# A two-block layer: where scan, gated unit and half of a projection stand among the attention heads

## The chip, the cores and the metric

The kernel runs on one core of one Trainium2 chip. The number that counts is the device time of one execution in microseconds (us), as the median over runs. The kernel is one program: a first transformer block (feed-forward, token mix, feed-forward) and a second block (attention and a state-space scan side by side, then a feed-forward with a convolution). 512 tokens of 1024 features; all in fp32, where most products are made as three products of high and low parts (fp32r).

## The reference, cut to what matters

The change touches only the middle of the second block:

```python
o_attn = nsa_attention(...)     # 8 heads of 64: 512 features; two dense causal branches and a compressed one, gated
y_ssm = s5_mixer(...)           # 512 features
    # inside: x = associative_scan(...); y = C x + d_skip * u
    #         y = gelu(y); y = y * sigmoid(y @ w_glu + b_glu)
mix = concatenate([rmsnorm(o_attn, attn_norm_g), rmsnorm(y_ssm, ssm_norm_g)], axis=-1)
x = x + gt1 * (mix @ w_o)
h = rmsnorm(x, norm2_g) * (1.0 + sc2) + sh2
u = causal_dwconv(h @ w_up, conv_w, conv_b)      # ... the feed-forward follows
```

Features 0 to 511 of `mix` are the attention's (k-tiles 0 to 3 of `w_o`), features 512 to 1023 the state-space output's (k-tiles 4 to 7).

## The kernel before, in words

Tiles are feature-major: 128 features on the partitions, 512 tokens in the free dimension. A weight block is loaded on the SP queue into `wraw`, copied to `whi` on ScalarE (L200) and subtracted to `wlo` on VectorE (L201); `mm3` then makes, for each k-tile, the products hi x hi (L212) and hi x lo (L213), and last lo x hi (L215).

The order of the instructions on each engine is made beforehand by a scheduler. Code order is an instruction's rank; `rank(-150)` moves what it encloses 150 places ahead. Tiles in SBUF and PSUM come from pools; a tile that reuses bytes waits for the earlier users of these bytes.

PSUM has banks of three kinds: four "a", two "p", two "t". In the attention, scan banks ("s") and a head pair's output bank ("o") are both of kind "p" (`self.kinds = dict(s="p", o="p")`). Scores, the gated unit's sums and the projection's sums are "a"; the transposed probabilities and the norm's row sums are "t".

`attn_heads` goes over four pairs of heads; each has two branches `br`. A branch computes, for two heads, scores (L1899) in a bank, their maximum (L1902), the exponential (L1908), a scaling by the gate on GpSimd (L1915), transposes (L1918), copies out (L1923, L1925) and at its end products with the values into `po` (L1931, L1936). After both branches `po` is copied to `oT` (L1938).

`s5_scan` is a generator with two steps for each quarter of the groups. A quarter loads its constants, copies its input to `z3` (L1608), transposes it (L1611, bank `pt`), copies it (L1613), multiplies (L1623, bank `pin`), rotates and scans on VectorE (L1628 to L1641), multiplies (L1652, bank `py`), adds (L1654), transposes back (L1657, another `pt`) and copies to `yT` (L1658). All four banks are "s".

Before the change `between(p)` runs one quarter ahead of each pair:

```python
for p in range(4):
    between(p)                 # next(s5); next(s5); at p == 3 also closes the scan's pool
    po = self.bank("o", [N, T])
```

After all pairs comes, under `rank(-150)`, the gated unit `glu`: gelu of four tiles (L2003), their split (L1231, L1232), four blocks of 12 products of 512 columns with `w_glu`, each with a sigmoid (L2010) and a product (L2011), and then the norm of the gated output (`mix2_norm` with `g_ssm`: squares L361, sums L363, L369, root L390, reciprocal L391, rows L379 and L381, scaling L1951, split L1231 and L1232).

`block2_merge` makes the same norm of the attention's output, and then `out_proj`: for the two halves of 256 tokens, eight output tiles `n`; each takes 24 products of 256 columns (k-tiles 4 to 7 first), a residual update (L1304), a square and a sum for the next norm (L361, L363). The weights of two tiles are held between the halves, so 14 blocks of 512 KB are loaded and split. After each half come the next norm's rows and the modulated operands (L422, L423), and the feed-forward's first products (L480, L481, L484).

Of the kernel before, what the change touches and what calls it, by code (L numbers as in the profile page):

```python
# [18 lines left out]
KT = 8  # L19
# [119 lines left out]
class Net:  # L139
# [16 lines left out]
    def pool(self, **k):  # L156
        """A pool whose tiles wait only for the earlier users of their own bytes."""
        if k.get("space") != bass.MemoryType.DRAM:
            k["reuse_waits"] = "tile"
        return self.tc.tile_pool(**k)  # L160
# [24 lines left out]
    def bank(self, group, shape=(128, 512)):  # L185
        """A PSUM bank of a kind: "a" (four), "p" and "t" (two each); self.kinds maps other names of a phase to them."""
        k = self.kinds.get(group, group)
        return self.pp.tile(list(shape), F32, tag=k, name=self.nm("ps" + group), bufs=dict(a=4, p=2, t=2)[k])
# [18 lines left out]
    def mm3(self, ps, w, x, last=0):  # L207
        """ps = sum_k w[k]^T x[k]; w, x: lists of (hi, lo) operand pairs over k-tiles. The low parts of w
        (or of x, with last=1) come into play last."""
# [12 lines left out]

    def ada_dot(self, w, ci):
        """sum_k c[k] * w[:, k] over the k-tiles of a [128, KT, 256] block: still to be summed over partitions."""
        nc = self.nc
        acc = self.tp.tile([128, 256], F32, tag="adaacc", name=self.nm("adaacc"), bufs=3)
        nc.vector.tensor_scalar(acc, w[:, 0], self.cs[:, ci, 0:1], None, ALU.mult)
        for k in range(1, KT):
            nc.vector.scalar_tensor_tensor(acc, w[:, k], self.cs[:, ci, k : k + 1], acc, ALU.mult, ALU.add)  # L229
        return acc  # L230

    def ada_dot2(self, w, ci, pool):
        """The same with products on ScalarE and sums on GpSimd."""
# [14 lines left out]
    def ada_finish(self, accs, outs, bias, chunk, b, tag):  # L248
        """Column sums over partitions, plus bias: outs[i][:, 2b : 2b + 2]."""
# [9 lines left out]
    def ada_product(self, w, outs, bias, chunk, b, tag):  # L259
        """Modulations by the first two vectors of c from a [128, KT, 256] block, with TensorE: outs[i][:, 2b : 2b + 2]."""  # L260
# [13 lines left out]
    def block_sum(self):  # L274
        """A stationary operand that sums over the partitions p with the same p % 32."""
# [5 lines left out]
    def ada_steps(self, src, bias, jobs, tag, done=None):  # L281
        """Small steps of the modulation vectors: jobs are (chunk, cids, outs); done(chunk) after its last block."""
# [9 lines left out]
        def sums(acc, part):  # L292
            """Sums over groups of 32 partitions, those partitions then being the columns within a group."""
# [4 lines left out]
        def finish(c, part, outs):  # L298
            """Sums over the groups of partitions, plus bias: outs[i] over all blocks."""
# [32 lines left out]
    def rank(self, n):  # L332
        """Instructions that the scheduler is to rank n places lower (higher if negative)."""
# [15 lines left out]

    def ssq(self, width, pool=None, tag="tok"):  # L350
        """Running sum of squares over features; see ssq_add and ssq_rstd."""
# [3 lines left out]
    def ssq_add(self, st, src, sl, k, eng=None, scale=1.0):  # L355
        """Adds k-tile k (columns sl)."""
# [8 lines left out]
    def ssq_cols(self, st, sl, ps):  # L365
        """Sums over features, tokens on partitions: one column of ps for each 128 tokens of sl."""
# [7 lines left out]
    def token_rows(self, rs, cols, sl, ps):  # L374
        """rs[:, sl] = the values of cols (tokens on partitions) along every partition."""
# [7 lines left out]
    def ssq_rstd(self, st, sl, ps):  # L383
        """1 / rms of columns sl, on every partition."""
# [15 lines left out]
    def new_xm(self, es):  # L400
        """Space for the (hi, lo) pairs of the modulated norm of x."""
# [8 lines left out]
    def norm_tile(self, xm, x, rs, a, sh, k, sl, pool=False):  # L410
        """(hi, lo) of (x * rs) * a + sh for k-tile k, columns sl."""
# [14 lines left out]
    def norm_mod(self, xm, xr, rs, a, sh, sls, dve=(0, 2, 4, 6)):  # L426
        """Operand pairs of the modulated norm, by column ranges in the order of sls."""
# [12 lines left out]
    def ffn(self, segs, w_in, w_out, act=None, group0=None, tail=None, nlast=2):  # L440
        """segs: (xm pairs over k, width, residual tiles, gate): residual += gate * swiglu(xm).
        group0: PSUM tiles of the first group when its products are already issued.
        tail(si, n, sl): called as the last group updates columns sl of residual tile n."""
# [17 lines left out]
        def stage_in(gi):  # L461
            hs = [[] for _ in segs]
            for jj, j in enumerate((gi * 2, gi * 2 + 1)):
# [8 lines left out]
                if j == 0:  # L472
                    # column halves and k-tiles in the order in which the norm delivers them
# [41 lines left out]
        def finish(gi, hs):  # L515
            """Output of the last nlast groups, by column halves, each with its tail."""
# [72 lines left out]
    def ffn1_start(self, xm, cm, segs, sp):  # L589
        """Modulation, norms and the first group's products, in steps of two k-tiles as the weights arrive."""  # L590
# [32 lines left out]
        # the square root's table is loaded while x arrives  # L623
# [12 lines left out]
        # the context's two accumulators of a bank share one group, opened by a product with zeros  # L636
# [53 lines left out]

    def mix_consts(self):
        """Masks of the two-level causal structure."""
# [34 lines left out]
    def gate_bounds(self):  # L727
        """Per-channel constants of the gates."""
# [21 lines left out]
    # fm column tiles of mix_fm  # L750
# [6 lines left out]
    def proj(self, w, seg, halves=False, tag="p"):  # L757
        """Feature-major projection of a segment ('x' or 'c') into a PSUM tile."""
# [7 lines left out]
    def vproj(self, src, bias, pool, tag, ones_col, nbs=range(4), bufs=6):  # L766
        """Token-major values: list of 6 chunk tiles [128 tok, heads, 128 (+2)]."""
# [40 lines left out]
    def hgrn_dir(self, h, d, q):  # L808
        """Gates of one head and direction; returns reference-shifted q, k, block products, ctx k, ctx/full decays."""
# [19 lines left out]
        def two(t, i0, i1):  # L829
            """Slots (i0, i1) of the inner index, in that order."""  # L830
# [31 lines left out]
        # block products: pre (ahead of the block's shifted reference) and suf (behind it), per level  # L862
# [23 lines left out]
        # context keys decayed to the end of the scan  # L886
# [12 lines left out]
    def hgrn_head(self, h, v):  # L899
# [18 lines left out]
        # mixed operands per level: half-blocks where the forward (backward) pairs live  # L918
# [36 lines left out]
        # states ahead of each chunk  # L955
# [43 lines left out]
    def mlstm_rows(self, rp):  # L999
        """Gate recurrences on rows (0:8 forward heads, 32:40 backward heads in reversed time)."""  # L1000
# [57 lines left out]
        # token-major scalars  # L1058
# [16 lines left out]
        # rows of M, natural time, as an exact hi + lo pair  # L1075
# [11 lines left out]
        # decays per (pair, direction, step), broadcast to the partitions of each head  # L1087
# [136 lines left out]
    def split(self, pool, tag, src, bufs):  # L1224
        """Exact hi + lo pair of a [128, T] tile."""
# [8 lines left out]
    def mix_heads(self, w):  # L1234
        """Normed, gated heads, feature-major: hi/lo pairs of hm and hh."""
# [54 lines left out]
    def out_proj(self, name, xs, gate, a, sh, ks=range(KT)):  # L1290
        """Residual += gate * (W xs), then its modulated norm, by column halves."""
# [3 lines left out]
        for sl in self.HALVES:  # L1295
            # the second half begins with the weights that the first one ended with
            for i, n in enumerate((6, 7, 0, 1, 2, 3, 4, 5) if sl.start else range(KT)):
                h, l = held.pop(n) if n in held else self.weights(self.ins[name][n], [KT, 128])
# [65 lines left out]
    def final_rstd(self, st, sl):  # L1364
        """For y = x * g / rms(x): 1 / rms(x), and 1 / (rms(x) * rms(y)) = 1 / sqrt(m2 + eps * (m1 + eps)),
        with m1, m2 the mean squares of x and x * g."""
# [33 lines left out]

    def s5_tables(self, w, tag):
        """Per group, for chunks of 8 steps: input, output and within-chunk matrices, and the rotation of the
        chunk-to-chunk recurrence; parked in DRAM. States lie on partitions, two groups to a tile."""
# [40 lines left out]
        def cmul(o, a, b):  # L1444
            """o = a * b for small complex pairs; o may not alias."""
# [9 lines left out]
        # f = (a - 1) / lam  # L1455
# [16 lines left out]
        # C as (real, -imaginary), each group's channels padded to 32 columns  # L1472
# [12 lines left out]
        # rotation tables e^(i 8 theta j)  # L1485
# [33 lines left out]
        # a^(7-t) B, a^(t+1) C on (state, step, channel)  # L1519
# [58 lines left out]
    def s5_scan(self, z2, wl, yT):  # L1578
        """z2: inputs [64 chunks, 8 steps, 512] in DRAM; writes gelu(S5(z)) feature-major into yT[4] ([128, T]).
        A generator: one quarter of the groups per step."""  # L1580
# [23 lines left out]
        for q in range(4):  # L1604
# [38 lines left out]
            # the groups of a pair lie on different parts of the array, and run side by side  # L1643
# [28 lines left out]
    def rope(self, ps, w):  # L1672
        """Rotary embedding of a feature-major tile (two heads of 64)."""
# [11 lines left out]
    def vtok2(self, nb, pool=None):  # L1685
        """Token-major projection of 256 columns: after its weights, two PSUM tiles [128, 2 chunks, 256]."""
# [12 lines left out]
    def token_pairs(self, x, w):  # L1699
        """[128 (2 heads x 64), T] with even and odd tokens on the two halves of the partitions."""  # L1700
# [7 lines left out]
    def compress(self, xk, xv, w):  # L1708
        """Block MLPs of token pairs: transposed hidden activations [128, 2, 128] (keys, then values from column 64)
        and the second layers' weights. The first layers lie on different columns of the array, and run side by side."""  # L1710
# [31 lines left out]
    def attn_operands(self, wl, w):  # L1742
        """Operands that the attention of all heads needs."""
# [5 lines left out]
        # keys and values of the two dense branches  # L1749
# [14 lines left out]
        # compressed keys and values  # L1764
# [318 lines left out]
```

## Time and profile before

| what | before |
|---|---|
| median of 3 runs (lowest, highest) | 2657.37 us (2654.51, 2658.23) |
| span of the profiled execution | 2655.4 us |
| busy, PE (TensorE) | 2548.3 us (96%) |
| busy, PEld (weight load, beside PE) | 2160.2 us (81%) |
| busy, DVE (VectorE) | 1671.0 us (63%) |
| busy, ACT (ScalarE) | 1095.8 us (41%) |
| busy, POOL (GpSimd) | 671.8 us (25%) |
| read from HBM | 261.30 MB |

The profile is one execution, taken by the hardware profiler; its span, 2655.4 us, is 2.0 us under the median of the runs. Times in the rows below count from the span's start. The granted clock of TensorE is given as a share of full speed (2.4 GHz; the lower level is 1.2 GHz).

### The profile page before, as it was taken

How to read it: one execution, taken by the hardware profiler on the slowest of the kernel's cores; microseconds unless marked ns; L12 is line 12 of the kernel's file. 1: busy time of each engine (PE TensorE's matmuls, PEld its weight loads, DVE VectorE, ACT ScalarE, POOL GpSimd, SP SyncE). 2: the span in 40 equal slices, each digit the busy share in tenths (PEclk: the TensorE clock that was granted, in tenths of full speed). 3: DMA queues.
4: the chain of work that ended last, by engine and by line, in shares of the span. 5: the costliest groups of instructions: out<-in, count | busy, mean ns of one | idle time of the engine just before them, and what ended most of it. 6: DMA issues, size and time to landing. Idle time of an engine off the chain costs nothing.

```text
span 2655.4 us, 38845 instructions
## 1 busy us (share of the span) xinstructions
PE 2548.3 (96%) x15220; PEld 2160.2 (81%) x15220; DVE 1671.0 (63%) x3123; ACT 1095.8 (41%) x2039; POOL 671.8 (25%) x683
## 2 busy tenths in 40 slices
PE   6999999999999999999999998999989999999998
PEld 4888888899988888897888887888786668888887
DVE  8756554436499995425433499986565777766665
ACT  6666631236233332415322352223343466533333
POOL 3677630012044344314000012006132350100001
PEclk8999999999999999999999999999989999999999
DMA  6344631221211111111333364654414223333332
GB/s 258 112 135 147 215 107 56 80 72 68 80 46 43 42 40 41 37 56 49 100 111 93 118 205 163 212 194 148 150 54 142 59 64 105 113 94 95 96 96 72
DMA packets 87878, 276.39 MB, mean 104 GB/s; under 512 B 12864, under 2 KB 31056, under 8 KB 79504
## 3 DMA queue, kind: packets, MB, share of 16 engines
q1 hardware_dynamic: 84912, 263.43, 31.4%
q0 software_dynamic: 2064, 7.35, 0.7%
q10 hardware_dynamic: 720, 3.15, 0.3%
q8 instruction: 119, 1.95, 0.3%
q14 instruction: 63, 0.52, 0.1%
HBM read 261.30 MB, written 12.59 MB: 103 GB/s over the span
## 4 chain that ended last, share of the span: by engine, by line
PE 79%; DVE 11%; ACT 4%; POOL 2%; issue 2%; DMA 1%; SPq 0%; DVEq 0%; POOLq 0%; ACTq 0%
PE psa L212 7%; PE psa L215 7%; PE psa L213 7%; PE psp L212 7%; PE psp L213 7%; PE psp L215 6%; PE psu L212 5%; PE psu L215 4%; PE psu L213 4%; PE pso L212 4%; PE pso L213 4%; PE pso L215 4%; DVE adaacc L229 1%; DVE wlo L201 1%; PE psc L212 1%
## 5 line engine op out<-in xcount | busy, mean ns | idle before, releaser
L201 DVE TENSOR_TENSOR wlo<-wraw,whi 128x1024 fp32r<-128x1024 f32 (+1 forms) x341 | 448.4, 1319 | 277.7 <-ACT whi L200 138.8
L200 ACT ACTIVATE whi<-wraw 128x1024 fp32r<-128x1024 f32 (+1 forms) x341 | 354.6, 1053 | 517.1 <-PE psp L213 156.7
L212 PE MATMUL psp<-xmh,whi 128*128 128x512 f32 (+1 forms) x760 | 286.5, 383 | 3.4 <-ACT K L823 3.1
L213 PE MATMUL psp<-xml,whi 128*128 128x512 f32 (+1 forms) x744 | 278.8, 381 | 0.0
L212 PE MATMUL psa<-xmh,whi 128*128 128x512 f32 x496 | 197.4, 398 | 1.4 <-ACT whi L200 1.4
L212 PE MATMUL psu<-xmh,whi 128*128 128x512 f32 x496 | 196.9, 397 | 0.8 <-ACT whi L200 0.8
L213 PE MATMUL psa<-xml,whi 128*128 128x512 f32 x496 | 196.0, 395 | 0.7 <-DVE xml L424 0.3
L213 PE MATMUL psu<-xml,whi 128*128 128x512 f32 x496 | 195.1, 393 | 0.0
L363 POOL TENSOR_TENSOR ssum<-ssum,sq 128x256 f32<-128x256 f32 x40 | 31.1, 777 | 641.1 <-ACT sq L361 640.8
L212 PE MATMUL pso<-hh,whi 128*128 128x512 f32 (+1 forms) x512 | 185.4, 368 | 4.4 <-DVE xr L507 4.2
L213 PE MATMUL pso<-hl,whi 128*128 128x512 f32 (+1 forms) x512 | 184.7, 366 | 0.0
L239 ACT ACTIVATE ap<-araw,cs 128x256 f32<-128x256 f32 x360 | 153.2, 498 | 66.8 <-POOL ap L242 46.8
L212 PEld LDWEIGHTS psp<-xmh,whi 128*128 128x128 f32 x760 | 150.7, 198 | 30.3 <-ACT K L823 4.8
L215 PE MATMUL psp<-xmh,wlo 128*128 128x512 f32 (+1 forms) x744 | 173.8, 373 | 0.0
L213 PEld LDWEIGHTS psp<-xml,whi 128*128 128x128 f32 x744 | 147.7, 198 | 24.2 <-issue 0.6
L215 PEld LDWEIGHTS psp<-xmh,wlo 128*128 128x128 f32 x744 | 130.5, 190 | 29.2 <-issue 4.4
L215 PE MATMUL pso<-hh,wlo 128*128 128x512 f32 (+1 forms) x512 | 145.6, 365 | 0.0
L242 POOL TENSOR_TENSOR ap<-ap,ap 128x1024 f32<-128x1024 f32 x45 | 109.8, 2441 | 120.3 <-ACT ap L239 120.3
L507 DVE SCALAR_TENSOR_TENSOR xr<-pso,hgate,xr 128x512 f32<-128x512 f32 x128 | 94.8, 745 | 67.4 <-PE pso L215 66.9
L215 PE MATMUL psu<-xmh,wlo 128*128 128x512 f32 x496 | 128.9, 399 | 5.7 <-DVE wlo L201 5.7
L215 PE MATMUL psa<-xmh,wlo 128*128 128x512 f32 x496 | 128.7, 395 | 0.0
L215 PEld LDWEIGHTS psu<-xmh,wlo 128*128 128x128 f32 x496 | 93.7, 190 | 28.1 <-DVE wlo L201 6.2
(674 smaller groups left out, 6091.6 us busy)
## 6 DMA issues: line engine op xcount, KB each, us to landing
araw<-in_ada_w_dram SPq DMA_DIRECT2D x60, 1024.0 KB, 5.7
wraw<-in_ffn_in_dram SPq DMA_DIRECT2D x88, 512.0 KB, 4.0
wraw<-in_mix_fm_dram SPq DMA_DIRECT2D x65, 512.0 KB, 3.6
wraw<-in_ffn_out_dram SPq DMA_DIRECT2D x44, 512.0 KB, 3.6
wraw<-in_up_dram SPq DMA_DIRECT2D x44, 512.0 KB, 3.7
wraw<-in_down_dram SPq DMA_DIRECT2D x22, 512.0 KB, 3.6
wraw<-in_mix_out_dram SPq DMA_DIRECT2D x14, 512.0 KB, 3.6
wraw<-in_w_o_dram SPq DMA_DIRECT2D x14, 512.0 KB, 3.7
```

What stands on the lines that cost most here:

```text
L200: nc.scalar.activation(hi, raw, AF.Copy)
L201: nc.vector.tensor_tensor(lo, raw, hi.bitcast(F32), ALU.subtract)
L212: self.nc.tensor.matmul(ps, wh, xh, start=k == 0, stop=False)
L213: self.nc.tensor.matmul(ps, *((wl, xh) if last else (wh, xl)), start=False, stop=False)
L215: self.nc.tensor.matmul(ps, *((wh, xl) if last else (wl, xh)), start=False, stop=k == n - 1)
L229: nc.vector.scalar_tensor_tensor(acc, w[:, k], self.cs[:, ci, k : k + 1], acc, ALU.mult, ALU.add)
L239: nc.scalar.activation(t[:, k], w[:, h * 4 + k], AF.Copy, scale=self.cs[:, ci, h * 4 + k : h * 4 + k + 1])
L242: nc.gpsimd.tensor_tensor(t, t, p[1], ALU.add)
L363: (eng or nc.vector).tensor_tensor(acc, acc, t, ALU.add)
L507: nc.vector.scalar_tensor_tensor(res[n], p, gt[:, n : n + 1], res[n], ALU.mult, ALU.add)
```

## The change

The side work is made one generator, `side()`, and is asked for once per branch, after the pair's `po` is taken. Calls 1 to 4 (pairs 1 and 2) run the four scan quarters. Call 5 (third pair, first branch) closes the scan's pool and runs the gated unit up to the gated tiles. Call 6 (third pair, second branch) runs the norm of the gated output. Calls 7 and 8 (fourth pair) run a new function, `out_part`, for output tiles 0 to 3 and 4 to 7: it loads the half of `w_o` that belongs to the state-space output (256 KB), splits it (128 x 512), makes 12 products of 512 columns into an "a" bank and adds them, times the gate, to the residual tile. `rank(-150)` is gone. `out_proj` is left with the k-tiles of attention: 12 products of 256 columns in each of its 16 groups, loads of 256 KB, splits of 128 x 512. Its call for the first block is the same as before. The remaining hunks of the diff only drop comments and docstrings.

```diff
-    def out_proj(self, name, xs, gate, a, sh, ks=range(KT)):
+    def out_proj(self, name, xs, gate, a, sh):
+        ks = range(len(xs))
...
-                h, l = held.pop(n) if n in held else self.weights(self.ins[name][n], [KT, 128])
+                h, l = held.pop(n) if n in held else self.weights(self.ins[name][n][:, : len(xs)], [len(xs), 128])
...
     def attn_heads(self, ops, w, oT, between):
...
         for p in range(4):
-            between(p)
             po = self.bank("o", [N, T])
...
             for br in range(2):
+                between()
...
-                s5 = self.s5_scan(z2, es.enter_context(self.pool(name="s5l", bufs=2, side="right")), yT)
-
-                def between(p):
-                    next(s5)
-                    next(s5)
-                    if p == 3:
-                        for _ in s5:
-                            pass
-                        es.close()
-                        self.new_xm(self.xs2)
-                        self.tp = self.glus.enter_context(self.pool(name="glu", bufs=2, side="right"))
-                self.attn_heads(ops, w, oT, between)
-                with self.rank(-150):
-                    self.glu(yT)
+                def side():
+                    s5 = self.s5_scan(z2, es.enter_context(self.pool(name="s5l", bufs=2, side="right")), yT)
+                    for _ in range(4):
+                        next(s5)
+                        next(s5)
+                        yield
+                    for _ in s5:
+                        pass
+                    es.close()
+                    self.new_xm(self.xs2)
+                    self.tp = self.glus.enter_context(self.pool(name="glu", bufs=2, side="right"))
+                    yield from self.glu(yT)
+                    for n in range(KT):
+                        self.out_part("w_o", 4, n, self.sm, self.mod2[:, 2])
+                        if n == 3:
+                            yield
+                sd = side()
+                self.attn_heads(ops, w, oT, lambda: next(sd, None))
+                for _ in sd:
+                    pass
+
+    def out_part(self, name, k0, n, xs, gate):
+        h, l = self.weights(self.ins[name][n][:, k0 : k0 + 4], [4, 128])
+        pp = self.bank("a")
+        self.mm3(pp, [(h[:, k], l[:, k]) for k in range(4)], xs)
+        self.nc.vector.scalar_tensor_tensor(self.xk[n], pp, gate[:, n : n + 1], self.xk[n], ALU.mult, ALU.add)
...
     def glu(self, yT):
...
+        yield
         self.sm = self.mix2_norm(yT, "g_ssm", pool, "ysp", 8)
+        yield
...
     def block2_merge(self):
...
-            xs = self.mix2_norm(self.oT, "g_attn", cat, "cat", 8) + self.sm
-            self.out_proj("w_o", xs, self.mod2[:, 2], self.coef(self.v("g_n2"), self.mod2[:, 4]), self.mod2[:, 3],
-                          (4, 5, 6, 7, 0, 1, 2, 3))
+            xs = self.mix2_norm(self.oT, "g_attn", cat, "cat", 8)
+            self.out_proj("w_o", xs, self.mod2[:, 2], self.coef(self.v("g_n2"), self.mod2[:, 4]), self.mod2[:, 3])
```

## Rows read from the trace of the kernel before

**Rows 1.** Windows from:to; busy us of each engine, granted clock, DMA share, GB/s.

```profile
core 0: us, PE busy (x) PEld busy (x) DVE busy (x) ACT busy (x) POOL busy (x), PEclk, DMA share, GB/s
2080.00:2104.00 24.00, 20.01 (x165) 14.25 (x165) 18.05 (x50) 12.60 (x34) 13.53 (x22) 0.86 0.32 81
2104.00:2176.00 72.00, 70.62 (x742) 52.72 (x738) 53.04 (x149) 43.94 (x113) 35.16 (x50) 1.00 0.25 75
2176.00:2191.00 15.00, 11.47 (x87) 7.50 (x85) 10.91 (x34) 7.58 (x24) 7.93 (x9) 0.89 0.20 56
...
2212.00:2226.00 14.00, 10.01 (x50) 9.47 (x49) 10.90 (x32) 10.10 (x29) 0.00 (x0) 0.63 0.17 59
2226.00:2272.00 46.00, 44.99 (x377) 44.46 (x377) 37.71 (x70) 28.38 (x53) 4.06 (x4) 1.00 0.45 133
...
2080.00:2290.00 210.00, 194.01 (x1685) 159.34 (x1684) 153.40 (x373) 126.79 (x295) 66.79 (x92) 0.95 0.30 89
```

**Rows 2.** Timeline of TensorE in the scan: start us, us, instruction, idle before it.

```profile
2106.97 0.71 PE L1657 MATMUL pss<-ident,zq 64*128 64x64 f32 x8
2107.60 1.08 PE L1931 MATMUL pso<-PC,vb 128*64 128x512 f32 x4
...
2112.08 0.71 PE L1611 MATMUL pss<-ident,z 64*128 64x64 f32 x8
...
2115.70 1.15 PE L1623 MATMUL pss<-u,s5i 128*64 128x64 f32 x32
...
2125.72 0.43 PE L1652 MATMUL pss<-s5o,S 64*64 64x128 f32 x4
...
2129.47 0.65 PE L1652 MATMUL pss<-s5o,S 64*64 64x128 f32 x8
...
2132.23 0.71 PE L1657 MATMUL pss<-ident,zq 64*128 64x64 f32 x8
...
2191.58 0.71 PE L1657 MATMUL pss<-ident,zq 64*128 64x64 f32 x8
```

**Rows 3.** Timeline of ScalarE: copies of the scan, one sigmoid, the last pair's copy.

```profile
2087.72 0.60 ACT L1613 ACTIVATE u<-pss 128x512 f32<-128x512 f32 x1 [0.32 <-PE pss L1611]
2088.29 1.06 ACT L1608 ACTIVATE z<-zq 64x1024 f32<-64x1024 f32 x1
...
2204.60 0.69 ACT L2010 ACTIVATE yg<-psa,vec 128x512 f32<-128x512 f32 x1
...
2213.47 0.57 ACT L1938 ACTIVATE oT<-pso 128x512 f32<-128x512 f32 x1
```

**Rows 4.** Timeline of VectorE: first quarter's instructions, and the last quarter's copy.

```profile
2090.16 0.69 DVE L1628 TENSOR_TENSOR xs<-pss,s5r 128x512 f32<-128x512 f32 x1
2090.77 0.68 DVE L1629 TENSOR_TENSOR xt<-pss,s5r 128x512 f32<-128x512 f32 x1
...
2109.32 1.09 DVE L1658 COPY oT<-pss 128x512 f32<-128x512 f32 x1
...
2193.03 1.09 DVE L1658 COPY oT<-pss 128x512 f32<-128x512 f32 x1
```

**Rows 5.** Groups from 2080 to 2220: instruction, count, busy us, mean ns.

```profile
L2003 ACT ACT_TABLE_LOAD x4 | 5.1, 1283 | 0.1
L1908 ACT ACT_TABLE_LOAD x4 | 5.1, 1283 | 0.1
```

**Rows 6.** The chain that ended last: eight products of 256, then of 512 columns.

```profile
2257.24 0.95 PE psa L215 x8
...
2291.04 1.87 PE psa L215 x8
```

**Rows 7.** Timeline of TensorE: first product of the projection, and of the feed-forward's second half.

```profile
2220.63 0.99 PE L212 MATMUL psa<-cat,whi 128*128 128x256 f32 x3
...
2281.07 0.38 PE L480 MATMUL psa<-xmh,whi 128*128 128x256 f32 x1 [2.10 <-ACT xmh L423]
```

**Rows 8.** Groups from 2226 to 2290: VectorE's split of the weights.

```profile
L201 DVE TENSOR_TENSOR wlo<-wraw,whi 128x1024 fp32r<-128x1024 f32 x14 | 17.2, 1226 | 1.4 <-ACT whi L200 1.4
```

## The prediction

> **What bounds the kernel now.** I first read the table by stage [rows 1], because the change touches one stretch of about 210 us out of 2655.4: attention beside the scan, the gated unit, the two norms and the output projection, from 2080 us until the feed-forward products start. Over it TensorE is busy 194.01 of 210.00 us, VectorE 153.40, ScalarE 126.79. So TensorE bounds nearly everywhere, and what there is to win lies in its gaps: 4.0 us in the first window, 3.5 us at 2176 to 2191, and 4.0 us at 2212 to 2226, where the granted clock is 0.63 of full speed, between the two levels of 1.2 and 2.4 GHz. The long window from 2104 has 70.62 busy of 72.00: four head pairs and the scan mixed, with no gap.
>
> Next I read how the scan and the heads share TensorE [rows 2]. A quarter of the scan is one group of transposes L1611, products L1623, products L1652 and transposes L1657. The four quarters end with L1657 at 2106.97, 2132.23, and so on to 2191.58: 25.3 us for the second, 59.35 for the last two together.
>
> The decisive reading is why the second quarter starts when it does. ScalarE has its input z ready at 2088.29 + 1.06 = 2089.35 [rows 3]. VectorE has read the first quarter's `pin` bank by 2090.77 + 0.68 = 2091.45 [rows 4], so one of the two "p" banks is free. Yet the transposes L1611 run only at 2112.08 [rows 2], after the copy L1658 has emptied the first quarter's last bank (2109.32 + 1.09 = 2110.41) [rows 4]. And the pair's output bank, asked for in the code just behind that last bank, sees its first product L1931 at 2107.60, right behind L1657 [rows 2]. I read this as: banks of a kind are handed out in the order in which the code asks for them; one that is free goes to nobody whose turn has not come. This decides my forecast.
>
> **The change, part by part.**
>
> *The order of banks.* After the change the code asks for the gated unit's four "a" banks before the third pair's scores, which also live in the four "a" banks. These are the last four before that pair, so its first scores need the first gate block's bank back, which needs all four scan quarters. Likewise the norm of the gated output stands ahead of the third pair's second branch ("t" banks, with its transposes), and the projection parts ahead of the fourth pair's two branches ("a"). Pairs 1 and 2 run beside two quarters, and then TensorE has the other two quarters alone.
>
> *Step 1: to the third quarter.* Two quarters as now: the second's L1657 at 2132.23, plus the 3.4 us from L1657 to the end of L1658 in the first (2106.97 to 2110.41), is 2135.6; say 2136 with the start of the next transposes.
>
> *Step 2: two quarters nearly alone.* Before, one takes 25.3 us beside attention (2106.97 to 2132.23): the upper end. Its own instructions in line give the lower end: eleven of VectorE from L1628 at 2090.16 to L1658 at 2109.32, 8.7 us together; ScalarE's copy L1613, 0.60; TensorE's 0.71, 1.15, 2.8 (five groups L1652, 2125.72 to 2129.47) and 0.71: 14.7 us. Waits between some 20 hand-overs and the low clock that an unfilled TensorE showed [rows 1] come on top, so I take 20.5, the middle: 41 us, to 2177.
>
> *Step 3: the gate.* From the last quarter's copy (2193.03 + 1.09 = 2194.12) [rows 4] to the end of the first gate block's sigmoid L2010 (2204.60 + 0.69 = 2205.29) [rows 3] are 11.2 us, the upper end. Nothing of attention stands in ScalarE's way now; two table loads of 1.28 [rows 5], gelu, two splits, some products and the sigmoid, each near 0.65, are 5.9: the lower end. I take 7, since the chain has one engine at a time: 2184. Only then do the third pair's scores start.
>
> *Step 4: TensorE's work left.* A pair and a quarter fill 25.3 us densely; less the quarter's 5.4 of TensorE a pair is 19.5 (at 70.62 of 72.00 busy), so two are 39. The eight projection parts have 12 products of 512 columns each; eight such took 1.87 us where eight of 256 took 0.95 [rows 6], so 0.234 and 0.119 each: 96 x 0.234 = 22.5. Rest of the gate 4 (up to 10, if its other blocks wait whole), norm products 2. That is 67.5. Gaps: the first window lost 4.0, and such a start comes again; the last branch has no filler behind it. I take 7 (3 to 16). Attention's output is copied at about 2258.5, where it was 2213.47 + 0.57 = 2214.04 [rows 3].
>
> *Step 5: attention's norm.* From that copy to the first projection product were 6.6 us (2220.63 [rows 7]), the two norms mixed; one alone I put at 7 (5.5 to 8, as it now has no other half to begin with): 2265.5.
>
> *Step 6: the projection.* From 2220.63 to the feed-forward's second-half product L480 at 2281.07 were 60.4 us [rows 7]. Removed: 192 products of 256 columns, 192 x 0.119 = 22.8 of TensorE, and half of each weight split L201, 14 x 1.226 / 2 = 8.6 of VectorE [rows 8]. VectorE had 37.71 in the 46 us of that window [rows 1]; 29.1 stay, against 44.99 - 22.8 = 22.2 of TensorE. So VectorE becomes the bound and the stretch gives back not 22.8 but 46 less 28 (some of the norm can go earlier): 18 (15 to 22.8). It takes 42.4, and ends at 2307.9, 26.8 later than 2281.07. The loads, 256 KB instead of 512, lie beside it: DMA share there 0.45 [rows 1]. The eight additional residual updates and eight split pairs of the parts run on VectorE while TensorE has the parts' products; without that cover they would be 8 x 1.4 = 11 us.
>
> *Everything behind* is as before. *The sum:* 2655.4 + 26.8 = 2682.2 in the profiled execution's own time. The median of the runs is 2657.37, 2.0 above its span, so 2684 us.
>
> *Table loads.* Four loads stand at the gelu and four at the exponentials between 2080 and 2220 [rows 5]; the change can add three to five where exponentials and sigmoids alternate, 3.9 to 6.4 us of ScalarE. It is busy 126.79 of 210 us, so I count none; uncovered they would cost 6.4. By the Trainium skill ("ScalarE: Activation LUTs", What ACT_TABLE_LOAD costs) a switch of table set is 1283 ns and a drain, about 2.66 us in all; by that figure five would be 13 us and the time, uncovered, 2697. The trace agrees with the 1283 ns and shows no drain: the sum goes by 1.28.
>
> **The rivals.**
>
> *B, faster.* The banks do not hold the third pair back (its scores L1899 run while a scan quarter is still at work, though the code asks later). Then gate and projection fill what is idle at 2176 to 2191 and 2212 to 2226, 3.5 and 4.0 us plus part of the low clock [rows 1]: about -8, so 2649. For it: 0.63 granted in that window. Against it: the second quarter's wait with a free bank. It decides if the third pair's first scores precede the last L1657. Beside this stands a rule of the Trainium skill ("Perfetto Trace Analysis", Optimization Strategy): where the most-contended engine changes between regimes, interleaving them may improve performance. It would be right here only if they did interleave.
>
> *C, within 0.2%.* With nothing of attention ahead of it in the code, the scan runs at its own pace from the start: four quarters of 16.4 (the 14.7 and 1.7 of hand-overs) from 2087 (L1613 at 2087.72 [rows 3]) end at 2153 and not 2177, with TensorE filled by the first two pairs until then (39 + 21.6 of work in 66 us). That gives 24 back: 2660. Against it: beside attention a quarter took 25.3 us at least.
>
> *D, slower still.* Two quarters without cover take 25.3 each, as before, +9.6, and the gaps are 12, not 7: +5; 2699. For it: VectorE and ScalarE hand over singly, at low clock.
>
> **How the numbers follow.** The forecast A has 0.60, D 0.15, C 0.11, B 0.14. A's own range, with half of each bound, is 2669 to 2698. Eight in ten must reach into C and D and leaves out B and D's far end: 2657 to 2702. Within 0.2% is within 5.3 us, about what a measurement of this kernel can tell from no change; so faster 0.14, same 0.11, slower 0.75.
>
> **What would show it.** Right: TensorE idle in stretches between about 2140 and 2184 with the clock granted below 1; the first L1899 of the third pair behind the first L2010; the second branch of that pair with L1918 behind the norm's L379; quarters 3 and 4 about 20 us each; the stage from attention's norm to the feed-forward's L480 shorter by about 18, with VectorE dense. Wrong: L1899 of the third pair between the third and fourth quarter's products (B), or L1657 of the fourth quarter by 2153 (C). The forecast fails above all if the order of banks is not the code's.

## The result and the profile after

The changed kernel takes 2698.81 us (median of 4 runs, 2693.61 to 2700.66); the kernel before took 2656.05 us beside it. The ratio is 1.0153, 95% interval 1.0136 to 1.0170: slower by some 41 to 43 us. The forecast was 2684 us, in a range from 2657 to 2702; the direction was right, the loss was put too small (27 us forecast).

The page of the changed kernel:

```profile
span 2698.9 us, 38704 instructions
PE 2563.7 (95%) x15124; PEld 2165.8 (80%) x15124; DVE 1676.3 (62%) x3139; ACT 1099.6 (41%) x2049; POOL 672.9 (25%) x683
```

TensorE's busy time grew by only 15.4 us (2548.3 before), the span by 43.5. So most of the added time is waiting of TensorE, and the rest, as the next view shows, goes into products at a lowered clock. Windows of the changed kernel, columns as in [rows 1]:

```profile
2136.00:2181.00 45.00, 29.88 (x304) 21.39 (x303) 22.33 (x41) 14.85 (x27) 12.45 (x9) 0.77 0.26 79
2181.00:2195.00 14.00, 13.66 (x53) 8.76 (x52) 6.25 (x10) 7.13 (x13) 0.00 (x0) 0.88 0.09 30
2195.00:2265.00 70.00, 59.80 (x387) 45.54 (x385) 42.40 (x120) 36.33 (x92) 14.56 (x24) 0.95 0.13 41
2265.00:2285.00 20.00, 12.61 (x91) 9.87 (x91) 12.20 (x38) 14.68 (x41) 4.79 (x8) 0.80 0.01 2
2285.00:2317.00 32.00, 27.16 (x207) 26.69 (x205) 27.04 (x56) 19.13 (x40) 2.87 (x3) 0.87 0.50 159
2080.00:2333.00 253.00, 208.53 (x1591) 163.74 (x1591) 159.44 (x391) 129.75 (x305) 67.10 (x92) 0.88 0.22 68
```

Where [rows 1] had 70.62 busy of 72.00, there are now 45 us with 29.88 busy and a granted clock of 0.77. No other engine is full there either: the stretch has too little to do. The reason stands in TensorE's timeline (in the attention and the scan, line numbers are one higher than before, in the gate 16 higher):

```profile
2109.52 1.08 PE L1932 MATMUL pso<-PC,vb 128*64 128x512 f32 x4
...
2136.86 0.71 PE L1612 MATMUL pss<-ident,z 64*128 64x64 f32 x8
...
2157.25 1.58 PE L1932 MATMUL pso<-PC,vb 128*64 128x512 f32 x4
2158.61 3.58 PE L1937 MATMUL pso<-PT,V 128*64 128x128 f32 x40
2162.12 0.71 PE L1612 MATMUL pss<-ident,z 64*128 64x64 f32 x8
...
2180.52 0.96 PE L212 MATMUL psa<-sp,whi 128*128 128x512 f32 x3
2181.83 3.49 PE L1932 MATMUL pso<-PC,vb 128*64 128x512 f32 x8 [0.34 <-DVE oT L1659]
...
2194.89 0.28 PE L1900 MATMUL psa<-kh,qs 128*128 128x256 f32 x1
...
2281.20 1.01 PE L212 MATMUL psa<-cat,whi 128*128 128x256 f32 x3 [0.99 <-ACT cat L1231]
...
2324.30 0.28 PE L480 MATMUL psa<-xmh,whi 128*128 128x256 f32 x1
```

The third quarter starts at 2136.86, the fourth at 2162.12; the third pair's first scores (L1900 at 2194.89) come only behind 44 of the gate's 48 products. On ScalarE, the first gate block's sigmoid and the copy of the last pair:

```profile
2191.45 0.69 ACT L2026 ACTIVATE yg<-psa,vec 128x512 f32<-128x512 f32 x1
...
2275.26 0.60 ACT L1939 ACTIVATE oT<-pso 128x512 f32<-128x512 f32 x1 [1.12 <-PE pso L1937]
```

That copy stood at 2213.47 [rows 3]; L480 of the second half, at 2281.07 [rows 7], is 43.2 us later, nearly the growth of the span (43.5), so what stands behind takes about as long as before.

### The profile page after: what moved, and what is told of

The parts are those of the page before. It is cut to its first block, busy times and chain, and to the rows that moved or that the text cites. A ratio compares the mean times of both kernels' runs of the same rounds, so it can differ in the third digit from the quotient of the medians.

```text
span 2698.9 us, 38704 instructions
## 1 busy us (share of the span) xinstructions
PE 2563.7 (95%) x15124; PEld 2165.8 (80%) x15124; DVE 1676.3 (62%) x3139; ACT 1099.6 (41%) x2049; POOL 672.9 (25%) x683
## 4 chain that ended last, share of the span: by engine, by line
PE 79%; DVE 11%; ACT 4%; POOL 2%; issue 2%; DMA 1%; SPq 0%; DVEq 0%; POOLq 0%; ACTq 0%
PE psa L212 7%; PE psa L213 7%; PE psa L215 7%; PE psp L212 7%; PE psp L213 6%; PE psp L215 6%; PE psu L212 5%; PE psu L215 5%; PE psu L213 5%; PE pso L212 4%; PE pso L213 4%; PE pso L215 4%; DVE wlo L201 1%; PE psc L212 1%; PE psc L215 1%
## 5 line engine op out<-in xcount | busy, mean ns | idle before, releaser
L507 DVE SCALAR_TENSOR_TENSOR xr<-pso,hgate,xr 128x512 f32<-128x512 f32 x128 | 95.0, 746 | 68.0 <-PE pso L215 67.5
```

The source lines that it names most:

```text
L507: nc.vector.scalar_tensor_tensor(res[n], p, gt[:, n : n + 1], res[n], ALU.mult, ALU.add)
```

## The experiments

**Theory T:** banks of a kind go to whoever asks first in the code; gate, norm and projection parts ask ahead of attention's third and fourth pairs, which wait. **Rival R:** the order itself, two quarters that have little beside them, costs the time whatever the banks. **Rival S:** the division of the projection costs it. Every kernel ran beside the kernel before; the ratio is to that. The runs of the kernel before differ from row to row, so two kernels are best compared by their ratios.

| kernel | median us | ratio, 95% interval |
|---|---|---|
| changed kernel | 2698.81 | 1.0153, 1.0136 to 1.0170 |
| e1_banks | 2671.39 | 1.0054, 1.0037 to 1.0071 |
| e2_split_only | 2663.05 | 1.0031, 1.0021 to 1.0041 |
| e3_order_only | 2687.11 | 1.0119, 1.0104 to 1.0135 |
| e4_po_first | 2698.27 | 1.0164, 1.0136 to 1.0192 |
| e5_order_banks | 2662.21 | 1.0023, 1.0013 to 1.0033 |
| e6_parts_last | 2673.43 | 1.0068, 1.0051 to 1.0085 |
| e7_gate_banks | 2689.67 | 1.0124, 1.0109 to 1.0139 |
| e8_behind_scores | 2696.36 | 1.0150, 1.0125 to 1.0174 |
| e9_half_divided | 2662.49 | 1.0023, 1.0014 to 1.0032 |
| e10_sums_pool | 2661.44 | 1.0017, 1.0008 to 1.0026 |
| e11_rest_banks | 2691.05 | 1.0135, 1.0119 to 1.0150 |
| e12_double_updates | 2662.57 | 1.0018, 1.0008 to 1.0027 |

**e1: other banks for the side work.** The order of the code is the changed kernel's.

```diff
-                self.kinds = dict(s="p", o="p")
+                self.kinds = dict(s="p", o="p", y="p")
...
-            ps = self.bank("a")          # glu
+            ps = self.bank("y")
...
-        pp = self.bank("a")              # out_part
+        pp = self.bank("y")
...
-        self.sm = self.mix2_norm(yT, "g_ssm", pool, "ysp", 8)
+        self.sm = self.mix2_norm(yT, "g_ssm", pool, "ysp", 8, "y")   # kind of the norm's banks, "t" otherwise
```

> The changed kernel, but the side work no longer asks for the banks of attention: the gate's four sums, the row sums of the gated output's norm and the eight projection parts take "p" banks instead of "a" and "t". Theory T (banks are handed out in the order of the code, and the gate's four "a" banks hold back the third pair): the third pair's scores run beside scan quarters 3 and 4, TensorE's idle stretch from 2140 to 2195 us (15 us of idle in 2136 to 2181, and a granted clock of 0.77) fills, and the time falls from 2699 by 20 to 30 us, to 2669 to 2679. Rival R (the two quarters run at their own pace and the work of the third pair stands behind them in rank anyway, whatever the banks): within 5 us of 2699.

2671.39 us: 27 us came back (26 by the ratios). TensorE's timeline and windows of e1:

```profile
2132.96 0.39 PE L1900 MATMUL psa<-kh,qs 128*128 128x256 f32 x1
...
2166.60 0.39 PE L1900 MATMUL psa<-kh,qs 128*128 128x256 f32 x1
```

```profile
2136.00:2160.00 24.00, 20.58 (x193) 15.68 (x194) 14.62 (x45) 12.51 (x32) 11.25 (x15) 0.86 0.21 67
2160.00:2181.00 21.00, 17.94 (x173) 12.63 (x169) 16.48 (x48) 13.74 (x38) 11.09 (x14) 1.00 0.23 64
```

The third pair's scores (the 33rd to 48th of 64 products L1900) start at 2132.96, 62 us earlier, the fourth pair's at 2166.60, and the same 45 us hold 38.5 of TensorE instead of 29.9. T holds for these 26 us and R falls for them: nothing but the kind of bank was changed.

**e2 and e3: the two halves of the change alone.** e2 is the kernel before with `out_part` and `out_proj` of the changed kernel, the parts behind the gate:

```diff
                 with self.rank(-150):
                     self.glu(yT)
+                    for n in range(KT):
+                        self.out_part("w_o", 4, n, self.sm, self.mod2[:, 2])
```

> The kernel before, with only the projection divided: the eight projection parts (512 columns) come behind the gated unit, at its rank, after all pairs, and the last projection keeps four k-tiles. Scan and gated unit stand as before. Theory T (the order costs, the division does not): the parts fill idle at 2212 to 2226 us and the last stage is 18 us shorter against 22.5 us of parts; 2648 to 2662. Rival S (the division itself costs: eight more residual updates of 0.75 us and more hand-overs on VectorE, not hidden): 2664 to 2680.

e3 is the changed kernel without the parts, its last projection over all eight k-tiles as before:

```diff
                     yield from self.glu(yT)
-                    for n in range(KT):
-                        self.out_part("w_o", 4, n, self.sm, self.mod2[:, 2])
-                        if n == 3:
-                            yield
```

> The changed kernel without the division of the projection: scan in the first two pairs, gated unit and its norm in the third, nothing in the fourth; the last projection takes all eight k-tiles as before. Theory T: the order of scan and gate carries the loss, so most of the 43 us stay: 2685 to 2700. Rival S (the division carries it): 2660 to 2670.

e3 has most of the loss (ratio 1.0119 of 1.0153), as T says. e2 has a loss of its own, 1.0031, about 8 us, between T's range and S's: this expectation had taken the division as free. So the order carries about three quarters, and the division is a second, small cost.

**e4: the output bank first.** The first products into `po` ahead of the side work:

```diff
+            for h, rows in heads:
+                mm(po[rows], VB[g][:, h % 4], PC[g], start=True, stop=False)
             for br in range(2):
                 between()
...
-                if br == 0:
-                    for h, rows in heads:
-                        mm(po[rows], VB[g][:, h % 4], PC[g], start=True, stop=False)
```

> The changed kernel, but each pair's first products into its output bank (L1932) are issued ahead of the side work instead of at the end of the first branch, so that this bank is taken first. In the changed kernel the second pair's output products wait until quarter 3 ends (2157.25 us) and then run ahead of quarter 4's transposes, which come 3.7 us after their bank is free; the third pair's L1932 runs 3.5 us ahead of the gate's products. Theory T (a bank is taken at its first product in code order): both waits go, 5 to 8 us faster than 2699, 2691 to 2694. Rival (only the scan's own chain counts there): within 3 us of 2699.

No gain (2698.27): T's time failed, and the rival's range holds the time. T's mechanism is there: in e4 these products (L1888 there) run at 2083.28 instead of 2109.52, and quarter 4 follows quarter 3 without the pair's products between. TensorE's timeline of e4:

```profile
2083.28 1.08 PE L1888 MATMUL pso<-PC,vb 128*64 128x512 f32 x4
...
2140.26 0.71 PE L1612 MATMUL pss<-ident,z 64*128 64x64 f32 x8
...
2160.92 1.11 PE L1612 MATMUL pss<-ident,z 64*128 64x64 f32 x8 [1.17 <-DVE oT L1659]
```

But quarter 3 starts 3.4 us later (2136.86 in the changed kernel), and the third pair's L1932 still runs ahead of most of the gate's products. That the delay comes from the pairs' products, which now lie beside the first two quarters, is likely but not shown. One thing e4 says for T: a bank's turn goes by its first product in the code. The line that names the bank stands at the same place in both kernels, and the bank is taken at another time.

**e5: the order without the division, with other banks.** e3 with e1's banks for gate and norm.

```diff
-            ps = self.bank("a")          # glu
+            ps = self.bank("y")          # kinds: y -> "p"; the norm's row sums too
```

> The undivided projection with the new order (e3, 2687 us), and the gate's sums and its norm's row sums in "p" banks. Theory T (the order of banks makes the loss): as from the changed kernel to e1, some 25 us less, 2655 to 2665, and the products with the state-space half again lie beside attention's norm. Rival R (the order itself costs, by its starved scan, and only the division gained from other banks): 2675 to 2690.

2662.21, 25 us under e3, as T forecast. With gate and norm in other banks the new order still costs 1.0023, some 6 us, and gains nothing against the order before; what makes these 6 us was not tested, and that much of R stays open. The pieces add up within their intervals: 0.23% here and 0.31% of e2 are the 0.54% of e1, and the rest of the 1.53%, about 1.0% or 26 us, is the banks.

**e6: parts kept for the end.**

```diff
-                        if n == 3:
+                        if n == 1 or n == 3:
                             yield
```

(on e1: parts 0 and 1, then 2 and 3 before the fourth pair's branches, the rest behind the last pair)

> As e1 (2671 us), with parts 4 to 7 of the projection left for behind the last pair, and parts 0 to 3 before its two branches by two. Theory U (once the state-space half is done early, nothing covers the end of the last branch and attention's norm; in e1 TensorE was idle 4.4 us of 20 there and the clock fell after): 4 to 9 us off, 2662 to 2667. Rival (the end is bound by VectorE and ScalarE, not by a lack of products): 2669 to 2674.

No gain against e1 (1.0068 and 1.0054, intervals that overlap). Theory U falls. The time lies in the rival's range, but that VectorE and ScalarE bind the end is not shown by it.

**e7 and e11: the holds one by one.** e7 moves only the gate's sums to "p" banks, e11 only the norm's and the parts'.

```diff
+            ps = self.bank("y")          # e7: in glu alone; e11: "a" here, "y" in mix2_norm and out_part
```

> The changed kernel with only the gate's four sums in "p" banks; norm and projection parts keep "t" and "a". Theory T, sized by the trace: the gate holds the longest (2140 to 2195 us), so at least two thirds of the 27 us that e1 gave come back here: 2675 to 2683. Rival: the norm ("t") or the parts ("a") hold as much, and the time stays at 2685 to 2699.

> The counterpart of e7: the changed kernel with the norm's row sums and the projection parts in "p" banks, and the gate's four sums still in "a". If the three holds add up, the 27 us of e1 less the 9 of e7: 2678 to 2684. If the gate's hold comes first and the others stand behind it (theory T as a chain, a later hold hides behind an earlier one): less than half of that, 2689 to 2697.

e7 gave back 9 us by the medians and 8 by the ratios, not 18 or more: the expectation of two thirds failed. e11 gave 8 and 5, in the range of a chain. The intervals of both overlap that of the changed kernel, that of e7 barely, so each gain by itself is near the noise. Both together (e1) gave 26 to 27, more than the two added: the holds are in a row, and what one lets go the next takes. The timelines of TensorE show it, first e7 and then e11:

```profile
2132.85 0.39 PE L1900 MATMUL psa<-kh,qs 128*128 128x256 f32 x1
...
2225.80 0.28 PE L1900 MATMUL psa<-kh,qs 128*128 128x256 f32 x1
```

```profile
2186.37 0.28 PE L1900 MATMUL psa<-kh,qs 128*128 128x256 f32 x1
```

In e7 the third pair starts at 2132.85, as in e1, but the fourth at 2225.80, behind the first four parts, where e1 has it at 2166.60. In e11 the third pair still waits for the gate, until 2186.37.

**e8: the same banks, another order.** The side work behind each branch's scores and transposes:

```diff
             for br in range(2):
-                between()
...
                     PT.append(pT)
+                between()
```

> The changed kernel, its banks unchanged, but each piece of side work stands behind the branch's scores and transposes in the code and ahead of its products with the values. Theory T (a bank goes to whoever asks first in the code): the third pair's first branch gets its "a" banks ahead of the gate and runs beside quarters 3 and 4; 2675 to 2688. Rival R (kinds of banks and their number count, not the order in the code): within 5 us of 2699.

No clear gain: 2696.36 lies outside T's range and in R's, and its interval holds that of the changed kernel. TensorE's timeline of e8:

```profile
2144.70 0.71 PE L1658 MATMUL pss<-ident,zq 64*128 64x64 f32 x8
2145.64 0.36 PE L1899 MATMUL psa<-kh,qs 128*128 128x256 f32 x1
...
2191.58 0.68 PE L1658 MATMUL pss<-ident,zq 64*128 64x64 f32 x8 [1.53 <-issue]
...
2209.19 0.39 PE L1899 MATMUL psa<-kh,qs 128*128 128x256 f32 x1
```

The order did what T says, and R's reason falls although its number held: with the same banks the third pair's first branch runs at 2145.64, ahead of the gate, and its second waits for the gate until 2209.19. But each quarter now stands behind a branch: the last ends with L1658 at 2191.58 instead of 2179.91. These 11.7 us, which T's number had not counted, are of the size of the TensorE work of the one branch that was moved ahead (half of the 19.5 that the prediction has for a pair); that they alone took the gain is not shown.

**e9, e10 and e12: why the division costs.** All on e2. In e2 the feed-forward's first products meet a lowered clock (windows of e2):

```profile
2226.00:2262.00 36.00, 36.00 (x230) 32.62 (x229) 26.38 (x52) 16.08 (x30) 0.00 (x0) 1.00 0.36 117
2262.00:2272.00 10.00, 8.34 (x62) 7.79 (x60) 9.25 (x18) 7.65 (x15) 2.37 (x3) 0.95 0.74 215
2272.00:2284.00 12.00, 9.82 (x46) 9.03 (x45) 6.53 (x13) 4.37 (x11) 2.42 (x3) 0.62 0.23 85
```

The kernel before has 9.90 of 12.00 at a clock of 1.00 in the last of these windows.

e9 divides only the first 256 tokens, and the second half takes all k-tiles again:

```diff
+            if divided and not sl.start:
+                ks = range(4)
...
+        sl = self.HALVES[0]                       # out_part: 256 columns
+        pp = self.bank("a")[:, :TC]
```

> As e2 (before's order, projection divided; 8 us slower than before, ratio 1.0031), but divided only for the first 256 tokens: the eight parts have 256 columns, the first half of the last projection four k-tiles, the second half all eight with weights of its own. Theory V (the division costs because the second half no longer covers the norm between the halves: in e2 the feed-forward's first products wait for their operands and then run at a lowered clock): the second half covers 22.8 us again, ratio 0.999 to 1.001. Rival W (the additional residual updates, loads and splits on VectorE cost it): they are as many or more here, ratio 1.003 or above.

e10 puts the sums on GpSimd:

```diff
-                self.ssq_add(st, r, sl, i)
+                self.ssq_add(st, r, sl, i, nc.gpsimd if len(xs) == 4 else None)
```

> As e2, with the 14 sums for the next norm (L363, 0.42 us each) in the last projection on GpSimd instead of VectorE. If VectorE's throughput sets the pace of the last projection (rival W): 2 to 5 us faster than e2, ratio 1.001 to 1.0023. Theory V (the chain through the norm between the halves, not VectorE's throughput): no gain, and GpSimd's slower sums lengthen the chain by 0 to 3 us, ratio 1.003 to 1.0045.

e12 makes the additional updates twice:

```diff
+        t = self.tp.tile([128, T], F32, tag="yg", name=self.nm("yg"))
+        self.nc.vector.scalar_tensor_tensor(t, pp, gate[:, n : n + 1], self.xk[n], ALU.mult, ALU.add)
         self.nc.vector.scalar_tensor_tensor(self.xk[n], pp, gate[:, n : n + 1], self.xk[n], ALU.mult, ALU.add)
```

> As e2 (ratio 1.0031), with each of the eight additional residual updates made twice, the first time into a scratch tile: 8 x 0.75 = 6 us more of VectorE beside the parts. If the additional updates are what the division costs (rival W), the cost grows by about as much again, ratio 1.0045 to 1.006. If they are covered and the division costs through the shorter last projection (its VectorE pace or its norm), ratio 1.002 to 1.004.

e12 did not grow (1.0018, just under the lower of its two ranges), though the sixteen updates took 11.9 us of VectorE: the additional updates are covered and aren't the cost. e9 (1.0023) fell into neither range, e10 (1.0017) into W's; the intervals of both overlap e2's. Windows of e9:

```profile
2272.00:2284.00 12.00, 10.25 (x86) 9.98 (x84) 8.25 (x16) 5.70 (x13) 1.55 (x2) 1.00 0.47 142
2284.00:2296.00 12.00, 11.10 (x57) 10.17 (x57) 5.82 (x12) 5.74 (x12) 2.57 (x4) 0.72 0.00 0
```

In e9 the second half does cover the norm, as theory V wants, and the clock is 1.00 up to 2284; but the low clock comes one window later, 0.72, and the time stays. VectorE's pace is not what holds e2 from 2226 to 2262, where TensorE has no gap (36.00 of 36.00) and VectorE 26.38; in the next 10 us VectorE is the fuller one, 9.25. So four kernels with a divided projection are slower by 0.17 to 0.31%, every interval above 1, and whether VectorE's pace in those few us or the low clock behind the norm makes it is not settled.

## Why the prediction was right in its way and short in its size

The mechanism that the forecast was built on, banks in the order of the code, is shown by e1 and e5, where 26 and 25 us come back by the kind of bank alone. Its size was short by 15 us: 2698.81 lies in the stated range, but just past the forecast's own 2669 to 2698 and on the 2699 of rival D, which gets there by other terms. Half of each step's bound, added without the table loads, gives 2672 to 2700, so even that inner range is not quite their sum. Step by step, forecast against the changed kernel's profile:

| step | ends at, forecast | ends at, measured | step's own error |
|---|---|---|---|
| 1 third quarter starts | 2136 | 2136.86 | +0.9 |
| 2 last quarter copied | 2177 | 2181.77 | +3.9 |
| 3 third pair's scores | 2184 | 2194.89 | +6.1 |
| 4 last pair copied | 2258.5 | 2275.86 | +6.5 |
| 5 first product of the projection | 2265.5 | 2281.20 | -1.7 |
| 6 L480 of the second half | 2307.9 | 2324.30 | +0.7 |

The errors add up to 16.4 us, which is 2324.30 less 2307.9. The last copy is seen on VectorE:

```profile
2157.36 1.08 DVE L1659 COPY oT<-pss 128x512 f32<-128x512 f32 x1 [0.81 <-PE pss L1658]
...
2180.63 1.14 DVE L1659 COPY oT<-pss 128x512 f32<-128x512 f32 x1 [0.82 <-PE pss L1658]
```

*Step 2* took 44.9 us and not 41 (the stated middle of 14.7 and 25.3 is 20.0, not 20.5, which hid 1 us of this). A quarter with little beside it does take about 20: the third, from 2136.86, is copied at 2158.44 (21.6 us), the fourth, from 2162.12, at 2181.77 (19.7 us). What I missed are the 3.7 us between them: the second pair's output bank came free behind quarter 3's last, and the pair's products (L1932, L1937, 2157.25 to 2162.12) went ahead of quarter 4's transposes on TensorE. So in a starved stretch there were still products, held by the same rule and let go at the wrong moment.

*Step 3* is the term most off for its length: 13.1 us where 7 were put. It took part of step 4 with it, since 44 of the 48 gate products ran in it, and the forecast had left 4 us of them to step 4. I assumed that most gate products could run before the last quarter is there. They did not: three of 48 stand ahead of the last copy (2180.52), then come eight products L1932 at the low clock, 3.49 us, and then the gate's products in one run until the scores slip in at 2194.89. The first sigmoid is done, and its bank free, at 2192.14 (2191.45 + 0.69); TensorE's own line of gate products holds the scores another 2.75 us.

*Step 4* took 81.0 us, 74.5 forecast. Windows of the changed kernel by the steps, step 4 and two parts of step 6, and of the kernel before for the whole of step 6:

```profile
2194.89:2275.86 80.97, 68.06 (x453) 51.65 (x451) 47.98 (x138) 44.03 (x116) 19.34 (x32) 0.94 0.11 36
2283.86:2309.04 25.18, 25.18 (x197) 25.14 (x197) 20.22 (x46) 13.49 (x29) 0.66 (x1) 0.93 0.45 144
2309.04:2324.30 15.26, 10.42 (x59) 9.99 (x58) 12.32 (x23) 9.66 (x21) 3.91 (x6) 0.66 0.33 108
```

```profile
2220.63:2281.07 60.44, 57.34 (x461) 56.61 (x461) 46.06 (x92) 33.42 (x67) 4.78 (x5) 0.96 0.41 123
```

The gaps are the term mis-sized: 12.9 us of idle (80.97 less 68.06) where 7 were put, in the stated 3 to 16. TensorE's busy time, 68.06, is near the 67.5 forecast, but about 3 us of gate products are no longer in it, and the granted clock is 0.94. The norm and the parts hold the second branch and the fourth pair, as the forecast said: that branch's transposes come behind the last L379 (2218.60), the fourth pair's scores at 2239.54, behind the first four parts. But I let this cost nothing beyond the ordinary gaps. e7 and e11 show that these holds weigh about as much as the gate's: with only the one or only the other left, the loss is 1.0124 or 1.0135, and 1.0054 with neither.

*Steps 5 and 6* came out near the forecast as times, step 6 by luck in its reason. The last projection gave back 17.3 us (60.4 before, 43.1 now) and not the 22.8 of TensorE; but VectorE did not become the bound. From 2283.86 to 2309.04 TensorE has no gap, 25.18 of 25.18, and VectorE is busy 20.22. What was not given back lies behind that, around the norm between the halves (10.42 of 15.26, at a clock of 0.66): over the step TensorE's busy time fell by 20.7 us (57.34 to 36.61) and its idle time grew by 3.4. Step 5 took 5.3 us, a little under its stated 5.5 to 8. The forecast had the division cost 4.5 us in sum (22.5 of parts less 18); e2 has it at 0.21 to 0.41%, some 6 to 11 us.

*The rivals.* B (faster) falls by its own mark: no score of the third pair precedes the last L1658. Where that mark is met, in e1 and e5, the gaps do not become a gain either: 1.0054 and 1.0023. The Trainium skill ("Perfetto Trace Analysis", Optimization Strategy) says that interleaving regimes may improve performance where the most-contended engine changes between them. There was no gain here even where the work did interleave, but TensorE bounds nearly the whole stretch before [rows 1], so its condition hardly holds. C falls: beside attention the scan kept its pace, with the second quarter's L1612 at 2112.72 and the third's 24.1 us later. D's longer gaps came (12.9 where it has 12), its slow quarters did not (21.6 and 19.7 where it has 25.3 each); that the time is D's number all the same is luck, since the gate's 6.1 us, which D does not have, stand in their place. The table loads from 2080 to 2325 are 12, before they were 10 from 2080 to 2290: two more, under the forecast's three to five, and ScalarE has room.

## What to carry to other kernels

Where tiles of one kind are handed out in code order, "beside" in the code is "ahead" in the queue: work that needs a late result and takes the same kind of bank stops what stands behind it, however free the engines are. Give such side work another kind than the work that it is to run beside, and look at every kind it touches, since here one freed hold mostly moved the wait to the next. That took back most of the loss and no more (1.0153 to 1.0054): no order tried here was faster than the one before. And before moving work into a stretch, see from its windows whether there is room: the one from 2104 had 1.4 us of idle in 72.

## What was not expected of the hardware

The clock makes the loss larger than the idle alone. Before, the stretch from 2080 to 2290 ran at a granted clock of 0.95 [rows 1]; the same work in the changed kernel, 2080 to 2333, has 0.88. Of the 43 us that this stretch grew, 28.5 are idle time of TensorE (44.5 now, 16.0 before) and 14.5 busy time (208.5 now, 194.0 before). The work did not grow: 96 products of 512 columns stand in for 192 of 256, which the prediction prices at 22.5 and 22.8 us. The lowered clock also reaches past the starved scan: in 2285 to 2317 it is 0.87, in the last projection, where before it was 1.00 (2226 to 2272). The forecast had counted a low clock only for the two quarters.
